# A fifth K-tile pair in seven block products in three of the four column passes of a down projection

## The chip, the cores and the metric

The kernel runs on one core of a Trainium2 chip. The metric is the time of one execution in microseconds on the device, the median of several runs. Trace times count from the start of the span of one profiled execution.

## The reference

A decoder layer on x of 256 tokens by 2048 channels in float32: a token mixer, then a channel mixer, each as x + post_norm(f(pre_norm(x))). The change lies in the channel mixer, and there in the last product:

```
h = rmsnorm(x, pre_ffn_g)
u = causal_dwconv(h @ w_up, conv_w, conv_b)          # 2048 -> 2 * 5632
gate, val = split(u, 2)
y = (gelu(gate) * val) @ w_down                      # 5632 -> 2048
x = x + rmsnorm(y, post_ffn_g)
```

## The kernel before

Every float32 operand of a matmul is split into a high part (a float32r cast, on ACT) and a low part (the rest, a subtraction on DVE), and a product is three matmuls: left high with right high, left high with right low, left low with right high. `split` (lines 311 to 313) makes the parts of the down projection's weights: the cast is L312, the subtraction L313. They go into the tiles whi and wlo, of which there are five each (`WB = 5`).

The hidden dimension of 5632 is done in two halves of 22 K-tiles of 128. A half first runs the up projection, the convolution and the gate for its 22 K-tiles, whose results stay as G (22 tiles, 256 tokens, high and low parts), and then its down projection: two column passes, n = 0 and n = 2, of 1024 output columns each. So there are four passes in all, two in each half. A pass goes through the 11 pairs of K-tiles, called pair 0 to pair 10 here. For a pair the two weight tiles ra and rb (128 rows by 1024 columns) are loaded; with two blocks of 128 tokens and two blocks of 512 columns a pair is a product of 2 x 2 by 2 x 2 blocks.

- A **plain** pair makes the eight block products as they stand: 24 matmuls with a moving operand of 512 columns, into four banks (late: p2, p3, p4, p22, one for each block of the result). It needs the parts of ra and rb: two casts and two subtractions, 1024 wide.
- A **fast** pair (those in FAST) makes seven block products, Winograd's form of Strassen's method: 21 matmuls, into the four late banks and four early ones (m1, m5, m7, m6). It needs sums of the token blocks, made once for each half by `token_sums` right after G and kept in sums, and differences of the weight blocks, made on DVE in each pass: t13 (L1007, L1008) and t24 (L1011, L1013), four operations 512 wide, in tb. It then splits b11 (half of ra, 512 wide), t13 into f13, t24 into f24 and rb into b2 (1024 wide). PE uses them in the order b11 (m1), f13 (m5, m7), f24 (m6, p4), b2 (p2, p3); in each product the high part comes first, the low part second.

The order of pairs is a table: 1, 3, 0, 5, 2, 7, 4, 8, 6, 9, 10 in a half's first pass and 0 to 10 in its second. After the last fast pair `add_early` adds the early banks to y_sb (four adds on DVE after a copy on ACT in half 0, L1116 to L1119; eight in half 1, L1123 to L1130). The last pair's products go block by block, and each block of the result is added to y_sb when it is done (L1149 in half 0; L1087 in half 1, with a square on ACT behind it). The last pass of all holds back its last three pairs (HOLD) and mixes them with the closing norm.

Weights are loaded by SP into eight places in turn: five raw tiles, two places in the tile extra, one in tb. tb shares its room with the tiles of the convolution ("room"), so it can be filled only when the half's convolution is over. Only PE's order is written out in this part of the code; the order on DVE, ACT, POOL and SP is set by a scheduler when the program is built.

Of the kernel before, what the change touches and what calls it, by code (L numbers as in the profile page):

```python
# [8 lines left out]
F32 = mybir.dt.float32  # L9
F32R = mybir.dt.float32r  # L10
BF16 = mybir.dt.bfloat16
AF = mybir.ActivationFunctionType
ALU = mybir.AluOpType
# [4 lines left out]
P = 128  # L18
S = 256
D = 2048  # L20
# [5 lines left out]
FHALF = 22  # L26
HOLD = 3
FAST = (0, 2, 4, 6)


@with_exitstack
def hybrid_layer(ctx: ExitStack, tc: tile.TileContext, x, pre_mix_g, w_in, b_forget, sinks,
# [31 lines left out]
    UNIT = 1024  # L64
# [782 lines left out]
    with tc.tile_pool(name="ffn", bufs=1) as fp:  # L847
# [105 lines left out]
        def token_sums(into, y0, y1):  # L953

            s = fp.tile([P, 4, P], F32, tag="cst", name="s")
            a11, a21 = y0[:, 0:P], y0[:, P:256]
            a12, a22 = y1[:, 0:P], y1[:, P:256]
            dve.tensor_tensor(s[:, 0, :], a21, a22, op=ALU.add)
            dve.tensor_tensor(s[:, 2, :], a11, a21, op=ALU.subtract)
            dve.tensor_tensor(s[:, 1, :], s[:, 0, :], a11, op=ALU.subtract)  # L960
            dve.tensor_tensor(s[:, 3, :], a12, s[:, 1, :], op=ALU.subtract)
            split(into[:, 0:512], into[:, 512:UNIT], s.rearrange("p k c -> p (k c)"))
# [6 lines left out]

        def fast_pass(G, sums, order, k00, c0, load, tb, early, late, add_early, hold=1,  # L970
                      keep=None):

            left, right = slice(0, 512), slice(512, UNIT)
            fast = [u for u in order if u in FAST]

# [18 lines left out]
            for u in order:  # L994
                k = 2 * u
                ra, rb = (load(w_rows(w_down, k00 + k + a, 1, c0, UNIT)) for a in range(2))
                if u in FAST:
                    i = FAST.index(u)
                    end = u == fast[-1]

                    def s_of(j):
                        return (sums[:, i, j * P:(j + 1) * P],
                                sums[:, i, 512 + j * P:512 + (j + 1) * P])

# [44 lines left out]
        for half in range(2):  # L1049
# [4 lines left out]
            for g in range(FHALF // 2):  # L1054
# [24 lines left out]
                if g in FAST:  # L1079
                    if sums is None:  # L1080
                        sums = main.tile([P, len(FAST), UNIT], F32R, tag="x", name="sums")
                    token_sums(sums[:, FAST.index(g), :], *ys)

# [5 lines left out]

            extra = fp.tile([P, 2, UNIT], F32, tag="gbc", name="extra")  # L1090
            tb = fp.tile([P, 3, UNIT], F32, tag="room", name="tb")
            spare = [extra[:, 0, :], extra[:, 1, :], tb[:, 2, :]]
            loads = [0]
# [9 lines left out]
            for n in (0, 2):  # L1103
                early, late = ([bank(tag) for _ in range(4)] for tag in ("acc", "att"))
                order = list(range(FHALF // 2))
                if n == 0:
                    order[:9] = [1, 3, 0, 5, 2, 7, 4, 8, 6]

# [25 lines left out]
                if final:  # L1134
                    rest = main.tile([P, 2, 2, UNIT], F32R, tag="hT", name="rest")
                block = fast_pass(G, sums, order, half * FHALF, n * 512, load, tb, early, late,
                                  add_early, HOLD if final else 1,
# [13 lines left out]
        def gain(t, n, h=None, into=None):  # L1151
            cs = slice(0, 512) if h is None else slice(h * 256, h * 256 + 256)
            ys = y_sb[:, t, n * 512:(n + 1) * 512][:, cs]
            pool.tensor_tensor(ys if into is None else into, ys,
                               gbf[:, n * 512:(n + 1) * 512][:, cs], op=ALU.mult)

# [24 lines left out]
        for t in range(2):  # L1181
            sp.dma_start(x_back[:, t, :], x_dram[t * P:(t + 1) * P, :])
        gbf = fp.tile([P, D], F32, tag="gbc", name="gbc_ffn")
        sp.dma_start(gbf, post_ffn_g[0].partition_broadcast(P))
        gain(0, 0)
# [61 lines left out]
```

## Time and profile before

| | us |
|---|---|
| median of three runs (1063.74 to 1064.3) | 1063.96 |
| the profiled execution | 1064.31 |
| its span | 1062.6 |
| PE busy | 1049.6 |
| DVE busy | 839.7 |
| ACT busy | 639.1 |
| down projection, half 0, first pass, from | 580.26 |
| half 1, first pass, from | 936.94 |

PE's busy time counts each matmul until it has drained, and these overlap; what one costs is the step from its start to the next one's. In a row of the order in time stand start, duration, engine, line, operation and how many were merged, and in square brackets how long the engine had been idle and what released it.

### The profile page before, as it was taken

The numbers are of one execution on the slowest core, as the hardware profiler recorded it, in microseconds if no ns is written. First come the engines' busy times: TensorE is split into PE (matmuls) and PEld (weight loads), VectorE is DVE, ScalarE is ACT, GpSimd is POOL, SyncE is SP. The second block draws the span as 40 slices with busy tenths as digits, with TensorE's granted clock in tenths as the row PEclk, the third lists the DMA queues.
The fourth block names the chain that finished last, engine by engine and source line by source line (L and its number), as shares of the span: only waits on it lengthen the run. The fifth ranks groups of instructions, "written<-read, shape, count | busy, mean of one in ns | idle before, by whom it ended". The sixth has DMA issues, their size and how long they took to land.

```text
span 1062.6 us, 16272 instructions
## 1 busy us (share of the span) xinstructions
PE 1049.6 (99%) x5890; PEld 914.6 (86%) x5890; DVE 839.7 (79%) x1369; ACT 639.1 (60%) x1096; POOL 229.3 (22%) x256
## 2 busy tenths in 40 slices
PE   9999999999999999999999999999999999999996
PEld 7889988888889888888888888888888888888885
DVE  5988887887467887787767999668778687789987
ACT  6767667776556765566655556446556565556551
POOL 4253335441022121211212000002121121200004
PEclk9999999999999999999999999999999999999998
DMA  8745566555773876656665666666566665656563
GB/s 280 217 120 168 162 209 202 165 170 162 282 236 107 280 231 187 193 180 185 211 188 188 193 204 206 213 196 190 169 209 188 197 197 180 194 179 200 194 242 121
DMA packets 154285, 207.08 MB, mean 195 GB/s; under 512 B 6845, under 2 KB 131037, under 8 KB 153181
## 3 DMA queue, kind: packets, MB, share of 16 engines
q1 hardware_dynamic: 153200, 203.37, 60.7%
q10 hardware_dynamic: 1004, 2.68, 0.6%
q8 instruction: 46, 0.75, 0.3%
q14 instruction: 35, 0.28, 0.1%
HBM read 201.68 MB, written 4.21 MB: 194 GB/s over the span
## 4 chain that ended last, share of the span: by engine, by line
PE 84%; DVE 9%; issue 2%; DMA 2%; ACT 2%; POOL 1%; DVEq 0%; SPq 0%; POOLq 0%; ACTq 0%
PE bank_acc L284 15%; PE bank_att L284 14%; PE bank_acc L309 12%; PE bank_att L967 9%; PE bank_acc L290 8%; PE bank_att L290 7%; PE bank_acc L253 7%; DVE wlo L313 4%; PE bank_acc L258 4%; PE bank_acc L967 2%; PE bank_att L475 1%; PE bank_att L510 1%; DVE wlo L115 1%; PE bank_acc L932 1%; DMA raw<-in_w_down_dram 1%
## 5 line engine op out<-in xcount | busy, mean ns | idle before, releaser
L115 DVE TENSOR_TENSOR wlo<-raw,whi 128x1024 fp32r<-128x1024 f32 (+3 forms) x271 | 328.5, 1224 | 127.0 <-ACT whi L112 118.4
L112 ACT CAST whi<-raw 128x1024 fp32r<-128x1024 f32 (+3 forms) x270 | 273.2, 1029 | 131.8 <-issue 88.8
L899 POOL TENSOR_TENSOR room<-room,rowf 128x256 f32<-128x256 f32 x88 | 100.3, 1160 | 393.9 <-DVE room L898 392.0
L284 PE MATMUL bank_acc<-hT,whi 128*128 128x512 f32 x736 | 173.3, 390 | 0.0
L284 PEld LDWEIGHTS bank_acc<-hT,whi 128*128 128x128 f32 x736 | 136.4, 188 | 27.4
L967 PE MATMUL bank_att<-whi,G 128*128 128x512 f32 x488 | 156.0, 389 | 0.0
L284 PE MATMUL bank_att<-hT,whi 128*128 128x512 f32 x640 | 150.6, 390 | 0.0
L284 PEld LDWEIGHTS bank_att<-hT,whi 128*128 128x128 f32 x640 | 118.7, 188 | 23.9
L967 PEld LDWEIGHTS bank_att<-whi,G 128*128 128x128 f32 x488 | 91.6, 188 | 18.9
L967 PE MATMUL bank_att<-wlo,G 128*128 128x512 f32 x244 | 95.0, 389 | 0.2 <-DVE wlo L313 0.2
L290 PEld LDWEIGHTS bank_acc<-hT,wlo 128*128 128x128 f32 x736 | 89.3, 188 | 2.0
L290 PE MATMUL bank_acc<-hT,wlo 128*128 128x256 f32 x736 | 89.8, 279 | 0.0
L901 ACT ACTIVATE room<-room,cw 128x256 f32<-128x256 f32 x88 | 53.0, 602 | 60.6 <-POOL room L899 60.6
L253 PE MATMUL bank_acc<-hT,whi 128*128 128x512 f32 x352 | 88.0, 395 | 0.0
L309 PE MATMUL bank_acc<-whi,oT 128*128 128x512 f32 (+1 forms) x272 | 81.7, 379 | 0.0
L290 PEld LDWEIGHTS bank_att<-hT,wlo 128*128 128x128 f32 x640 | 77.6, 188 | 1.7
L290 PE MATMUL bank_att<-hT,wlo 128*128 128x256 f32 x640 | 77.9, 279 | 0.0
L903 DVE SCALAR_TENSOR_TENSOR room<-room,cw 128x256 f32<-128x256 f32 x88 | 62.4, 709 | 17.6 <-ACT room L901 17.3
L253 PEld LDWEIGHTS bank_acc<-hT,whi 128*128 128x128 f32 x352 | 63.3, 188 | 11.5
L313 DVE TENSOR_TENSOR wlo<-raw,whi 128x1024 fp32r<-128x1024 f32 (+1 forms) x56 | 61.3, 1119 | 12.1 <-ACT whi L312 12.1
L312 ACT CAST whi<-tb 128x1024 fp32r<-128x1024 f32 x42 | 44.0, 1050 | 43.0 <-PE bank_att L967 19.6
L312 ACT CAST whi<-raw 128x1024 fp32r<-128x1024 f32 (+1 forms) x56 | 52.3, 958 | 27.1 <-PE bank_att L967 20.6
(254 smaller groups left out, 1594.0 us busy)
## 6 DMA issues: line engine op xcount, KB each, us to landing
raw<-in_w_up_dram SPq DMA_DIRECT2D x176, 512.0 KB, 4.2
raw<-in_w_down_dram SPq DMA_DIRECT2D x58, 512.0 KB, 4.7
raw<-in_w_in_dram SPq DMA_DIRECT2D x51, 512.0 KB, 4.7
raw<-in_w_out_dram SPq DMA_DIRECT2D x32, 512.0 KB, 4.6
extra<-in_w_down_dram SPq DMA_DIRECT2D x20, 512.0 KB, 4.7
raw<-in_w_in_dram SPq DMA_DIRECT2D x16, 384.0 KB, 3.6
tb<-in_w_down_dram SPq DMA_DIRECT2D x10, 512.0 KB, 3.5
cb<-c_dram SPq DMA_DIRECT2D x8, 256.0 KB, 3.8
```

The lines of the kernel that those rows point to most:

```text
L112: i1 = act.copy(hi[:, cs], raw[:, cs])
L115: i2 = dve.tensor_tensor(lo[:, cs], raw[:, cs], hi[:, cs].bitcast(F32), op=ALU.subtract)
L253: pe.matmul(b, parts[u][0][:, a, m * P:(m + 1) * P], hT[:, kt, :], start=(kt == 0), stop=(kt == KT - 1))
L284: pe.matmul(b, parts[u][0][:, a, m * P:(m + 1) * P], hT[:, kt, :], start=(kt == 0), stop=(kt == KT - 1))
L290: pe.matmul(b[:, 256:512], parts[u][1][:, a, m * P:(m + 1) * P], hT[:, kt, 0:256], start=False, stop=False)
L309: pe.matmul(b, a, r[:, cols], start=(first and i == 0), stop=(last and i == 2))
L312: act.copy(hi, src)
L313: dve.tensor_tensor(lo, src, hi.bitcast(F32), op=ALU.subtract)
L899: pool.tensor_tensor(u[:, 2:258], u[:, 2:258], rowf, op=ALU.mult)
L901: act.activation(y, u[:, 2:258], AF.Identity, bias=cw[:, 3, ch:ch + 1], scale=cw[:, 2, ch:ch + 1])
L903: dve.scalar_tensor_tensor(y, u[:, 1:257], cw[:, 1, ch:ch + 1], y, op0=ALU.mult, op1=ALU.add)
L967: pe.matmul(b[:, to] if to else b, a, r[:, cols], start=(first and i == 0), stop=(last and i == 2))
```

## The change

Pair 8 joins FAST. It is done in seven products in both passes of half 0 and in the first pass of half 1, while the last pass keeps four fast pairs. The first passes' order becomes 1, 3, 0, 5, 2, 7, 4, 9, 6, 8, 10: pairs 6 and 8 stand side by side, and add_early follows pair 8, with pair 10 alone behind it. The fifth pair's token sums get a tile of their own (sum5). Of the loads' three spare places one is in extra and two in tb now. The closing gain vector lies in two tiles and is loaded in two transfers.

```diff
--- before.py
+++ after.py
@@ -25,7 +25,7 @@
 NEG = -1e30
 FHALF = 22
 HOLD = 3
-FAST = (0, 2, 4, 6)
+FAST = (0, 2, 4, 6, 8)
 
 
 @with_exitstack
@@ -967,11 +967,11 @@
                 pe.matmul(b[:, to] if to else b, a, r[:, cols], start=(first and i == 0),
                           stop=(last and i == 2))
 
-        def fast_pass(G, sums, order, k00, c0, load, tb, early, late, add_early, hold=1,
+        def fast_pass(G, sums, some, order, k00, c0, load, tb, early, late, add_early, hold=1,
                       keep=None):
 
             left, right = slice(0, 512), slice(512, UNIT)
-            fast = [u for u in order if u in FAST]
+            fast = [u for u in order if u in some]
 
             def of(k, t):
                 return G[k][:, t * P:(t + 1) * P], G[k][:, 256 + t * P:256 + (t + 1) * P]
@@ -994,13 +994,13 @@
             for u in order:
                 k = 2 * u
                 ra, rb = (load(w_rows(w_down, k00 + k + a, 1, c0, UNIT)) for a in range(2))
-                if u in FAST:
-                    i = FAST.index(u)
+                if u in some:
+                    i = some.index(u)
                     end = u == fast[-1]
 
                     def s_of(j):
-                        return (sums[:, i, j * P:(j + 1) * P],
-                                sums[:, i, 512 + j * P:512 + (j + 1) * P])
+                        return (sums[i][:, j * P:(j + 1) * P],
+                                sums[i][:, 512 + j * P:512 + (j + 1) * P])
 
                     b11 = parts(ra[:, left], 512)
                     t13, t24 = tb[:, 0, :], tb[:, 1, :]
@@ -1077,9 +1077,13 @@
                     split(gt[:, 0:256], gt[:, 256:512], y)
                     ys.append(y)
                 if g in FAST:
-                    if sums is None:
-                        sums = main.tile([P, len(FAST), UNIT], F32R, tag="x", name="sums")
-                    token_sums(sums[:, FAST.index(g), :], *ys)
+                    i = FAST.index(g)
+                    if i == 0:
+                        first4 = main.tile([P, 4, UNIT], F32R, tag="x", name="sums")
+                        sums = [first4[:, n, :] for n in range(4)]
+                    elif i == 4:
+                        sums.append(fp.tile([P, UNIT], F32R, tag="sum5", name="sum5"))
+                    token_sums(sums[i], *ys)
 
             def down(t, n, b, h=None):
                 i, cs = (n, slice(0, 512)) if h is None else (n + h, slice(h * 256, h * 256 + 256))
@@ -1087,9 +1091,9 @@
                 dve.tensor_tensor(ys, b[:, cs], ys, op=ALU.add)
                 act.activation(junk[:, cs], ys, AF.Square, accum_out=ysq[t][:, i:i + 1])
 
-            extra = fp.tile([P, 2, UNIT], F32, tag="gbc", name="extra")
-            tb = fp.tile([P, 3, UNIT], F32, tag="room", name="tb")
-            spare = [extra[:, 0, :], extra[:, 1, :], tb[:, 2, :]]
+            extra = fp.tile([P, UNIT], F32, tag="extra", name="extra")
+            tb = fp.tile([P, 4, UNIT], F32, tag="room", name="tb")
+            spare = [extra, tb[:, 2, :], tb[:, 3, :]]
             loads = [0]
 
             def load(src):
@@ -1102,9 +1106,9 @@
 
             for n in (0, 2):
                 early, late = ([bank(tag) for _ in range(4)] for tag in ("acc", "att"))
-                order = list(range(FHALF // 2))
+                order, fast = list(range(FHALF // 2)), FAST[:4 if half and n else 5]
                 if n == 0:
-                    order[:9] = [1, 3, 0, 5, 2, 7, 4, 8, 6]
+                    order = [1, 3, 0, 5, 2, 7, 4, 9, 6, 8, 10]
 
                 def y_of(t, c):
                     return y_sb[:, t, (n + c) * 512:(n + c + 1) * 512]
@@ -1133,7 +1137,7 @@
                 rest = None
                 if final:
                     rest = main.tile([P, 2, 2, UNIT], F32R, tag="hT", name="rest")
-                block = fast_pass(G, sums, order, half * FHALF, n * 512, load, tb, early, late,
+                block = fast_pass(G, sums, fast, order, half * FHALF, n * 512, load, tb, early, late,
                                   add_early, HOLD if final else 1,
                                   rest and [[rest[:, a, i, :] for i in range(2)]
                                             for a in range(2)])
@@ -1152,7 +1156,7 @@
             cs = slice(0, 512) if h is None else slice(h * 256, h * 256 + 256)
             ys = y_sb[:, t, n * 512:(n + 1) * 512][:, cs]
             pool.tensor_tensor(ys if into is None else into, ys,
-                               gbf[:, n * 512:(n + 1) * 512][:, cs], op=ALU.mult)
+                               gbf[n // 2][:, n % 2 * 512:(n % 2 + 1) * 512][:, cs], op=ALU.mult)
 
         def before_last(t, n):
 
@@ -1180,8 +1184,9 @@
         x_back = main.tile([P, 2, D], F32, tag="x", name="x_back")
         for t in range(2):
             sp.dma_start(x_back[:, t, :], x_dram[t * P:(t + 1) * P, :])
-        gbf = fp.tile([P, D], F32, tag="gbc", name="gbc_ffn")
-        sp.dma_start(gbf, post_ffn_g[0].partition_broadcast(P))
+        gbf = [fp.tile([P, UNIT], F32, tag=tag, name="gbc_ffn") for tag in ("extra", "sum5")]
+        for i, g in enumerate(gbf):
+            sp.dma_start(g, post_ffn_g[0, i * UNIT:(i + 1) * UNIT].partition_broadcast(P))
         gain(0, 0)
         gain(0, 1)
         block(0)
```

Lines behind the diff's places move: L1087 becomes L1091, L1116 to L1119 become L1120 to L1123, L1123 to L1130 become L1127 to L1134, L1149 becomes L1153; L1007 to L1013, L312 and L313 keep their numbers.

On DVE, where half 1's first pass ends and pair 0 of the second pass is prepared, before (y_sb from s or bank_acc is add_early, y_sb from bank_att a block's add, wlo from extra b11 of pair 0, wlo from tb its f13 and then its f24, tb from raw a difference for pair 2):

```order
L1127 TENSOR_TENSOR s<-bank_acc,s 128x512
L313 TENSOR_TENSOR wlo<-extra,whi 128x512
L1128 TENSOR_TENSOR y_sb<-s,y_sb 128x512
L313 TENSOR_TENSOR wlo<-tb,whi 128x1024
L1129 TENSOR_TENSOR s<-bank_acc,s 128x512
L1087 TENSOR_TENSOR y_sb<-bank_att,y_sb 128x512
L1130 TENSOR_TENSOR y_sb<-s,y_sb 128x512
L1087 TENSOR_TENSOR y_sb<-bank_att,y_sb 128x512
L313 TENSOR_TENSOR wlo<-tb,whi 128x1024
L1087 TENSOR_TENSOR y_sb<-bank_att,y_sb 128x512
L1007 TENSOR_TENSOR tb<-raw 128x512
L1087 TENSOR_TENSOR y_sb<-bank_att,y_sb 128x512
```

There pair 0's four differences stood further up; f24 comes ahead of the last two block adds.

The same place now, from the middle of add_early on:

```order
L1131 TENSOR_TENSOR s<-bank_acc,s 128x512
L1091 TENSOR_TENSOR y_sb<-bank_att,y_sb 128x512
L1132 TENSOR_TENSOR y_sb<-s,y_sb 128x512
L1091 TENSOR_TENSOR y_sb<-bank_att,y_sb 128x512
L1133 TENSOR_TENSOR s<-bank_acc,s 128x512
L1091 TENSOR_TENSOR y_sb<-bank_att,y_sb 128x512
L1134 TENSOR_TENSOR y_sb<-s,y_sb 128x512
L313 TENSOR_TENSOR wlo<-tb,whi 128x1024
L1091 TENSOR_TENSOR y_sb<-bank_att,y_sb 128x512
L1011 TENSOR_TENSOR tb<-tb 128x512
L1008 TENSOR_TENSOR tb<-raw 128x512
L1013 TENSOR_TENSOR tb<-tb 128x512
```

b11 and one difference of pair 0 stand further up; f13 comes behind the whole of add_early and three block adds, and the other two differences of pair 0 (L1011, L1013), from which f24 is made, behind the fourth, with one of pair 2 (L1008) between them.

On DVE at the same place of half 0, before:

```order
L1118 TENSOR_TENSOR y_sb<-bank_acc,y_sb 128x512
L1119 TENSOR_TENSOR y_sb<-bank_acc,y_sb 128x512
L313 TENSOR_TENSOR wlo<-extra,whi 128x512
L313 TENSOR_TENSOR wlo<-tb,whi 128x1024
L1007 TENSOR_TENSOR tb<-raw 128x512
L1008 TENSOR_TENSOR tb<-raw 128x512
L1149 TENSOR_TENSOR y_sb<-bank_att,y_sb 128x512
L313 TENSOR_TENSOR wlo<-tb,whi 128x1024
L1149 TENSOR_TENSOR y_sb<-bank_att,y_sb 128x512
L1011 TENSOR_TENSOR tb<-raw,tb 128x512
L1149 TENSOR_TENSOR y_sb<-bank_att,y_sb 128x512
L1013 TENSOR_TENSOR tb<-raw,tb 128x512
```

f24 of pair 0 comes behind the first block add.

And now:

```order
L313 TENSOR_TENSOR wlo<-tb,whi 128x512
L1122 TENSOR_TENSOR y_sb<-bank_acc,y_sb 128x512
L1123 TENSOR_TENSOR y_sb<-bank_acc,y_sb 128x512
L1153 TENSOR_TENSOR y_sb<-bank_att,y_sb 128x512 x2
L313 TENSOR_TENSOR wlo<-tb,whi 128x1024
L1153 TENSOR_TENSOR y_sb<-bank_att,y_sb 128x512 x2
L1011 TENSOR_TENSOR tb<-tb 128x512
L1008 TENSOR_TENSOR tb<-raw 128x512
L1013 TENSOR_TENSOR tb<-tb 128x512
L1007 TENSOR_TENSOR tb<-raw 128x512
L313 TENSOR_TENSOR wlo<-tb,whi 128x1024 x2
L313 TENSOR_TENSOR wlo<-raw,whi 128x1024 x2
```

All four block adds stand ahead of pair 0's last differences and so of its f24.

On SP, at the start of half 1's down projection (the first place in extra is filled early, among the up projection's loads), before:

```order
L1100 DMA extra<-in_w_down_dram 128x1024 x2
L69 DMA raw<-in_w_up_dram 128x4x256 x87
L69 DMA raw<-in_w_down_dram 128x1024 x9
L1100 DMA tb<-in_w_down_dram 128x1024
L69 DMA raw<-in_w_down_dram 128x1024
L1100 DMA extra<-in_w_down_dram 128x1024 x2
L1100 DMA tb<-in_w_down_dram 128x1024
```

And now:

```order
L1104 DMA extra<-in_w_down_dram 128x1024
L69 DMA raw<-in_w_up_dram 128x4x256 x87
L69 DMA raw<-in_w_down_dram 128x1024 x9
L1104 DMA tb<-in_w_down_dram 128x1024 x2
L69 DMA raw<-in_w_down_dram 128x1024
L1104 DMA extra<-in_w_down_dram 128x1024
L1104 DMA tb<-in_w_down_dram 128x1024 x2
```

One of the two loads into extra has become a second one into tb, which waits for the convolution's room.

## The prediction

> **What bounds the kernel now.** I read the page first, then who waits for whom on PE, then the four column passes of the down projection as stretches, then the order in time of DVE, ACT and PE where one pass follows another.
>
> ```profile
> span 1062.6 us, 16272 instructions
> PE 1049.6 (99%) x5890; PEld 914.6 (86%) x5890; DVE 839.7 (79%) x1369; ACT 639.1 (60%) x1096; POOL 229.3 (22%) x256
> ...
> PE bank_acc L169 <- DVE junk L164: 1.3, 1, 1.3
> PE bank_att L522 <- DVE pl L313: 0.5, 1, 0.5
> ...
> PE bank_att L967 <- DVE wlo L313: 0.2, 1, 0.2
> ...
> 580.26:637.38 57.12, 57.12 (x253) 47.30 (x252) 53.98 (x70) 31.13 (x37) 1.79 (x2) 1.00 0.60 199
> 637.38:694.50 57.12, 57.12 (x253) 47.30 (x252) 44.49 (x48) 30.02 (x32) 0.20 (x4) 1.00 0.64 209
> 936.94:994.06 57.12, 57.12 (x253) 47.30 (x252) 54.23 (x70) 32.15 (x41) 1.79 (x2) 1.00 0.59 197
> 994.06:1050.70 56.64, 56.47 (x261) 46.94 (x260) 50.24 (x59) 28.27 (x36) 9.05 (x7) 1.00 0.50 181
> ```
>
> PE is busy 99% and waits 0.2 us in all for the down projection's parts, so each matmul removed is time gained and each new wait of PE is time lost. The last rows are the four passes (stretch, PE, PEld, DVE busy): in the first pass of either half DVE, which makes the low parts, is itself busy 53.98 and 54.23 of 57.12 us. It has 3.1 and 2.9 us free there.
>
> **What the change takes from PE.**
>
> ```profile
> 591.14 0.39 PE L967 MATMUL bank_acc<-whi,G 128*128 128x512 f32 x1
> ...
> 595.90 0.39 PE L967 MATMUL bank_att<-whi,G 128*128 128x512 f32 x1
> ...
> 601.34 0.39 PE L967 MATMUL bank_acc<-whi,G 128*128 128x512 f32 x1
> ```
>
> These are the first matmuls of pairs 0 (seven products), 5 (eight) and 2. Pair 0 takes 595.90 - 591.14 = 4.76 us for 21 matmuls, pair 5 takes 5.44 us for 24: 0.227 us each (the 0.39 is how long one is under way, not the step). Pair 8 loses three matmuls in three passes: 9 x 0.227 = 2.04 us, all on the path. That is the whole gain.
>
> **What it adds to DVE.**
>
> ```profile
> 972.95 1.23 DVE L313 TENSOR_TENSOR wlo<-tb,whi 128x1024 fp32r<-128x1024 f32 x1 [0.47 <-ACT whi L312]
> 975.48 0.69 DVE L1007 TENSOR_TENSOR tb<-extra 128x512 f32<-128x512 f32 x1 [1.31 <-DMA extra<-in_w_down_dram]
> ...
> 979.10 1.22 DVE L313 TENSOR_TENSOR wlo<-raw,whi 128x1024 fp32r<-128x1024 f32 x1
> 980.23 0.69 DVE L1013 TENSOR_TENSOR tb<-tb 128x512 f32<-128x512 f32 x1
> 980.83 1.22 DVE L313 TENSOR_TENSOR wlo<-raw,whi 128x1024 fp32r<-128x1024 f32 x1
> 981.97 0.69 DVE L1123 TENSOR_TENSOR y_sb<-s,y_sb 128x512 f32<-128x512 f32 x1
> ...
> 988.38 0.68 DVE L313 TENSOR_TENSOR wlo<-extra,whi 128x512 fp32r<-128x512 f32 x1
> 988.98 0.68 DVE L1128 TENSOR_TENSOR y_sb<-s,y_sb 128x512 f32<-128x512 f32 x1
> ...
> 993.11 1.22 DVE L313 TENSOR_TENSOR wlo<-tb,whi 128x1024 fp32r<-128x1024 f32 x1
> ...
> 996.05 1.21 DVE L313 TENSOR_TENSOR wlo<-tb,whi 128x1024 fp32r<-128x1024 f32 x1
> 997.18 1.22 DVE L313 TENSOR_TENSOR wlo<-raw,whi 128x1024 fp32r<-128x1024 f32 x1
> ```
>
> DVE from pair 6, the last fast pair of the first pass, to pair 0 of the second pass. Start to start, a 1024-wide operation takes 1.14 us and a 512-wide one 0.60. A plain pair costs DVE two of the first, 2.27 us; a fast one costs three, and five of the second (b11 and the four differences), 6.4 us. Pair 8 thus adds 4.1 us to DVE in each of three passes and gives it 0.68 us less time. Between the rows at 980.23 and 997.18 DVE never rests: seven wide and fifteen narrow operations, 7 x 1.135 + 15 x 0.60 = 16.95. Twelve of the narrow ones are adds of finished sums into y_sb: eight of add_early and one for each of the four blocks. How late is it there already?
>
> ```profile
> 994.06 0.39 PE L967 MATMUL bank_acc<-whi,G 128*128 128x512 f32 x1
> ...
> 996.33 0.39 PE L967 MATMUL bank_acc<-wlo,sums 128*128 128x512 f32 x1
> ...
> 997.69 0.39 PE L967 MATMUL bank_att<-wlo,G 128*128 128x512 f32 x1
> ...
> 639.00 1.22 DVE L313 TENSOR_TENSOR wlo<-tb,whi 128x1024 fp32r<-128x1024 f32 x1
> ...
> 641.01 0.39 PE L967 MATMUL bank_att<-wlo,G 128*128 128x512 f32 x1
> ```
>
> Pair 0's last low part, b2, is done at 997.18 and first used at 997.69 (half 1), done at 639.00 + 1.14 = 640.14 and used at 641.01 (half 0). The slack is 0.5 and 0.9 us. Before, pairs 9 and 10, both plain, stood between the last fast pair and this point; now only pair 10 does.
>
> **Can DVE run ahead?**
>
> ```profile
> 973.22 1.05 ACT L312 CAST whi<-tb 128x1024 fp32r<-128x1024 f32 x1 [0.31 <-PE bank_att L967]
> 975.90 1.06 ACT L312 CAST whi<-raw 128x1024 fp32r<-128x1024 f32 x1 [1.63 <-PE bank_att L967]
> ...
> 988.82 1.05 ACT L312 CAST whi<-tb 128x1024 fp32r<-128x1024 f32 x1 [1.66 <-PE bank_att L967]
> ```
>
> Each cast waits for PE to release one of the five whi buffers, so hardly. And DVE keeps its order: the cast of pair 6's f24 ended at 974.27, but its low part stood behind the difference that waited for a load until 975.48.
>
> Now the walk by the new order, with time 0 at pair 8's first matmul (983.18 in half 1's first pass: 936.94 + 41.48 for five plain and three fast pairs, + 4.76 for pair 6). From 974.09, where pair 6's f13 is done, eleven DVE operations lead to pair 8's b2: 5 x 1.135 + 6 x 0.60 = 9.3, and two waits of 0.5 for casts, because pair 9's last buffer comes free at 978.42; so b2 is done at +1.2. Loads don't stop DVE there any more: pair 8's lie in raw places filled long before. Pair 10's first part waits for its cast to 1.35. PE leaves pair 8 at 4.76, ends pair 10's blocks at 6.12, 7.48, 8.84 and 10.20, and then starts pair 0 of the second pass: m1, m5 (f13's low part due at 11.11), m7, m6 (f24's high part at 12.24, its low part at 12.47).
>
> Half 1. Ahead of f13's low part now stand pair 10's two wide operations, eleven adds, b11 and one difference: 1.35 + 2 x 1.135 + 13 x 0.60 = 11.4. It is done at 12.6, 1.5 us late. Behind it come the last block add, which has waited for block 4 of pair 10, and three differences, one of them for pair 2: 15.0. On ACT the cast of f24 stands behind four squares, the last one of that block add, done by 13.9; so it starts at 15.1 and ends at 16.15, and the low part at 17.35. PE, 1.5 us late, wants the high part at 13.75: 2.4 us of wait, and 1.0 more for the low part. Sum: 4.9 us.
>
> Half 0, where add_early has four adds on DVE. Two wide and eight narrow operations lead to f13: 1.35 + 2.27 + 4.8 = 8.5, its low part is done at 9.6, in time. Two block adds follow, the second held until block 4 ends (10.4): 11.0; three differences: 12.8; the cast of f24: 13.95; its low part: 15.15. PE waits 1.8 for the high part (due at 12.24, seen at 14.05) and 0.9 for the low one: 2.7 us.
>
> In half 0's second pass pair 8 is followed by 9 and 10, both plain, and DVE has 12.6 us free (57.12 - 44.49): nothing. **Sum: -2.0 + 4.9 + 2.7 = +5.6 us.**
>
> Bounds: if DVE could use all its idle time, half 1 lacks 4.1 + 0.6 (the moved difference) + 0.7 - 0.5 - 2.9 = 2.0 and half 0 4.1 + 0.6 + 0.7 - 0.9 - 3.1 = 1.4, so +1.4 in all; if it can use none, 4.9 and 4.5, so +7.4. I take the walk, since it keeps to the order and the buffers.
>
> **The small edits, costed at nothing.**
>
> ```profile
> 724.96 0.28 DVE L961 TENSOR_TENSOR s<-room,s 128x128 f32<-128x128 f32 x1
> ...
> 726.30 0.69 DVE L313 TENSOR_TENSOR sums<-s,sums 128x512 fp32r<-128x512 f32 x1
> ...
> 936.46 1.23 DVE L313 TENSOR_TENSOR wlo<-raw,whi 128x1024 fp32r<-128x1024 f32 x1 [2.85 <-ACT whi L312]
> ...
> 943.25 0.33 SPq L1100 DMA_DIRECT2D tb<-in_w_down_dram  x1
> ...
> DMA to landing us min/median/max: 3.5/3.5/6.0
> ...
> 1040.68 3.00 POOL L1154 TENSOR_TENSOR y_sb<-y_sb,gbc_ffn 128x512 f32<-128x512 f32 x2 [100.80 <-DMA gbc_ffn<-in_post_ffn_g_dram]
> ```
>
> The fifth token sums (four 0.2 us operations, one of 0.60 and a cast, once per half) go beside the up projection, where DVE rests up to 2.85 us a time; if that cover were gone they would cost 1.4 us a half. One more load waits for the conv room at a half's start (943.25); landing in 3.5 to 6.0 us it is there by 949.9, its cast by 951.0, and pair 5 starts on PE at 936.94 + 15.64 = 952.58: 1.6 us of cover. SP only keeps two more loads behind that release, none due sooner. In the second passes one raw place is now tb's, freed by pair 0's b2 and wanted for pair 4's difference: 0 to 0.6 us. The gain vector in two transfers lands no later than one.
>
> **Rivals.** (1) The adds give way and the gain stays: DVE's delay falls on y_sb, which nobody waits for, and f13 and f24 are in time. Then -2.0: 1061.9. It decides if f24's low part is done before 12.47 in half 1, five us earlier than walked. For it speaks PE's bare 0.2 us of waits now; against it the slack of 0.5 us and the rows in order. (2) The waits cost more, by the clock:
>
> ```profile
> 1051.19 0.88 PE L967 MATMUL bank_acc<-rest,G 128*128 128x256 f32 x6
> ...
> 1050.00:1055.00 5.00, 2.07 (x18) 1.86 (x16) 3.70 (x9) 1.74 (x6) 2.33 (x3) 1.00 0.51 195
> 1055.00:1058.00 3.00, 0.00 (x0) 0.00 (x0) 2.39 (x3) 0.00 (x0) 1.24 (x2) 0.51 0.10 41
> ```
>
> After PE's last matmul ended at 1052.07 the granted clock stayed 1.00 to 1055 and was 0.51 from there: about 3 us of rest halve it. My longest wait is 2.4 us, with three matmuls and 1.0 us of wait around it. Were it halved, the nine matmuls left of pair 0 would take 2.0 us more at each of the two places: +9.7, 1073.7. The Trainium skill ("TensorE: Matmul & The Clock Gate", Part 1) has the clock halved after an idle window of about 3.4 us that runs free of the kernel; by that rule a 2.4 us wait is safe, and 3.4 us with one matmul inside it may not be. (3) DVE runs further ahead than the ring lets it in my walk, say because casts start sooner after PE's release, and uses all its idle time: the lower bound, +1.4, 1065.4. Against it stand the 1.63 us that a cast waited for PE in the rows above.
>
> **How the numbers follow.** The profiled execution took 1064.31, 1.7 more than its span; the median of the runs is 0.35 lower, so 1063.96 + 5.6 = 1069.6. Chances: the walk 0.74, the clock 0.11, the lower bound 0.10, no waits 0.05. The range runs from the lower bound, 1063.96 + 1.4 = 1065.4, to a little beyond the upper bound, 1071.4, for one of two clock drops: 1072.6. A measurement of this kernel can tell about 0.2%, 2.1 us: slower by more 0.88 (the first two, and a third of the lower bound's), within it 0.09 (the rest of that, and half of rival 1, whose -2.0 lies at the edge), faster 0.03.
>
> **What would show it.** PE's list of waits should hold L967 waiting for DVE wlo and ACT whi of L312, about 7.6 us, near the starts of the two second passes and nowhere else; the first passes 56.4 us instead of 57.12; L967 nine matmuls fewer; DVE without a gap in those places. Wrong would be: no such waits, waits inside the first passes (pairs 6 and 8 side by side), or a granted clock under 1.00 there.

## The result, and the profile after

| | before | after |
|---|---|---|
| median, us | 1063.85 (6 runs, 1063.37 to 1064.30) | 1072.26 (6 runs, 1069.84 to 1074.45) |
| ratio of the times | | 1.0078, interval 1.0062 to 1.0094 |
| profiled execution, us | 1064.31 | 1073.85 |
| its span, us | 1062.6 | 1072.1 |

The change made the kernel 8.4 us slower, where 5.6 was forecast. The runs of after lie in three groups, each with its mean granted clock: 1069.84 and 1070.10 (0.996), 1072.18 and 1072.33 (0.994), 1073.85 and 1074.45 (0.991). The profiled execution is one of the last group.

The head of the page, and then who PE waits for (total, times, longest, in us):

```profile
span 1072.1 us, 16302 instructions
PE 1053.4 (98%) x5881; PEld 916.4 (85%) x5881; DVE 854.8 (80%) x1397; ACT 645.2 (60%) x1104; POOL 228.8 (21%) x256
```

```profile
PE bank_acc L967 <- ACT whi L312: 3.8, 2, 2.1
PE bank_acc L967 <- DVE wlo L313: 2.7, 3, 1.5
```

Nine matmuls fewer, 5881 for 5890, and 6.5 us of waits for the down projection's parts where there were 0.2. Where they are, in PE's order in time; first the start of half 0's second pass, then that of half 1's:

```profile
638.19 0.39 PE L967 MATMUL bank_acc<-whi,sums 128*128 128x512 f32 x1
640.28 0.50 PE L967 MATMUL bank_acc<-whi,sums 128*128 128x512 f32 x1 [1.70 <-ACT whi L312]
641.54 0.79 PE L967 MATMUL bank_acc<-wlo,sums 128*128 128x512 f32 x1 [0.76 <-DVE wlo L313]
642.13 0.63 PE L967 MATMUL bank_acc<-whi,sums 128*128 128x512 f32 x1
642.56 0.63 PE L967 MATMUL bank_att<-whi,G 128*128 128x512 f32 x1
...
1000.15 0.50 PE L967 MATMUL bank_acc<-wlo,sums 128*128 128x512 f32 x1 [1.46 <-DVE wlo L313]
1003.69 0.80 PE L967 MATMUL bank_acc<-whi,sums 128*128 128x512 f32 x1 [2.10 <-ACT whi L312]
1004.95 0.80 PE L967 MATMUL bank_acc<-wlo,sums 128*128 128x512 f32 x1 [0.46 <-DVE wlo L313]
```

These are the places of the forecast, f24's high and low part in half 0, f13's low part and both of f24's in half 1, and there are no others: no row of L967 inside a first pass has a wait. The reader should also see the steps behind the waits: from 642.13 to 642.56 a matmul takes 0.43 us, where it took 0.227 before.

DVE in half 1, from f13's low part (998.87) to f24's (1003.67):

```profile
998.87 1.23 DVE L313 TENSOR_TENSOR wlo<-tb,whi 128x1024 fp32r<-128x1024 f32 x1
1000.00 0.69 DVE L1091 TENSOR_TENSOR y_sb<-bank_att,y_sb 128x512 f32<-128x512 f32 x1
1000.60 0.69 DVE L1011 TENSOR_TENSOR tb<-tb 128x512 f32<-128x512 f32 x1
1001.20 0.70 DVE L1008 TENSOR_TENSOR tb<-raw 128x512 f32<-128x512 f32 x1
1001.80 0.70 DVE L1013 TENSOR_TENSOR tb<-tb 128x512 f32<-128x512 f32 x1
1002.40 0.70 DVE L1007 TENSOR_TENSOR tb<-raw 128x512 f32<-128x512 f32 x1
1003.67 2.36 DVE L313 TENSOR_TENSOR wlo<-tb,whi 128x1024 fp32r<-128x1024 f32 x2 [0.56 <-ACT whi L312]
```

It is the row of work that the walk counted: the last block add (L1091), three differences, of which one (L1008) is for the next fast pair, and then the wait for the cast. The fourth difference (L1007), which the walk did not have, falls into the time of that cast and so costs nothing; 0.56 us of the cast are left behind it.

The granted clock stands in the column ahead of the last two (stretch, its length, busy time of PE, PEld, DVE, ACT and POOL, PEclk, DMA share, GB/s). First after, half 0; then a kernel with the same two waits there (e2, below), in an execution in which the clock held:

```profile
642.00:648.00 6.00, 6.00 (x16) 4.61 (x16) 6.00 (x8) 2.63 (x4) 0.00 (x0) 0.53 0.57 175
```

```profile
642.00:648.00 6.00, 6.00 (x28) 4.97 (x27) 6.00 (x9) 2.17 (x3) 0.00 (x0) 1.00 0.63 195
```

From 640.87, inside the second wait, the clock of after was half for 6.8 us; in the stretch shown 16 matmul records stand where e2 has 28. In half 1 it was half from 1002.68 on, again for 6.8 us.

To tell the parts apart in each run, three lengths were read off each trace: the start of half 0's first pass; from there to half 1's first pass (before 936.94 - 580.26 = 356.68 us); and from there to DVE's last row (before 121.52). For half 1 these are the rows, of before and then of after, with the first of the closing 256-column matmuls:

```profile
1047.59 0.28 PE L967 MATMUL bank_acc<-whi,G 128*128 128x256 f32 x1
1058.46 0.47 DVE L1173 SCALAR_TENSOR_TENSOR y_sb<-last,ry,x_back 128x256 f32<-128x256 f32 x1
```

```profile
1057.99 0.28 PE L967 MATMUL bank_acc<-whi,G 128*128 128x256 f32 x1
1068.11 0.47 DVE L1177 SCALAR_TENSOR_TENSOR y_sb<-last,ry,x_back 128x256 f32<-128x256 f32 x1
```

Differences to before, in us:

| profiled execution | start | half 0 | half 1 | both halves |
|---|---|---|---|---|
| after | -0.32 | +4.56 | +5.41 | +9.97 |
| e12, after again | -1.22 | +3.15 | +4.84 | +7.99 |
| e1, fifth pair in half 0's second pass | -0.77 | -0.68 | +0.63 | -0.05 |
| e2, in half 0's first pass | -0.70 | +2.36 | +0.66 | +3.02 |
| e3, in half 1's first pass | -0.77 | +0.05 | +5.75 | +5.80 |
| e4, waits filled | -1.02 | +1.70 | +3.27 | +4.97 |
| e5, small edits alone | -0.66 | 0.00 | +0.55 | +0.55 |
| e6, seven adds left out | -0.81 | +1.67 | -2.09 | -0.42 |
| e7, differences on POOL | -0.40 | +0.87 | +3.38 | +4.25 |
| e8, and adds on POOL | +0.05 | +0.87 | +2.41 | +3.28 |
| e9, DVE's order | -0.73 | -0.91 | +4.87 | +3.96 |
| e10, order and sums | -0.96 | -0.95 | -0.49 | -1.44 |
| e11, two plain pairs behind | -0.04 | -0.49 | +1.88 | +1.39 |

The start differs from one execution to the next by up to 1.3 us, ahead of all the code that was touched.

### The profile page after: what moved, and what is told of

It is laid out like the page before. It is cut to its first block, busy times and chain, and to the rows that moved or that the text cites. A ratio compares the mean times of both kernels' runs of the same rounds, so it can differ in the third digit from the quotient of the medians.

```text
span 1072.1 us, 16302 instructions
## 1 busy us (share of the span) xinstructions
PE 1053.4 (98%) x5881; PEld 916.4 (85%) x5881; DVE 854.8 (80%) x1397; ACT 645.2 (60%) x1104; POOL 228.8 (21%) x256
## 4 chain that ended last, share of the span: by engine, by line
PE 92%; DVE 4%; ACT 1%; issue 1%; DMA 1%; POOL 1%; DVEq 0%; SPq 0%; POOLq 0%; ACTq 0%
PE bank_acc L284 16%; PE bank_att L967 15%; PE bank_att L284 14%; PE bank_acc L309 12%; PE bank_acc L290 8%; PE bank_att L290 7%; PE bank_acc L253 7%; PE bank_acc L967 4%; PE bank_acc L258 4%; PE bank_att L475 1%; PE bank_att L510 1%; DVE wlo L115 1%; PE bank_acc L932 1%; DVE wlo L313 1%; PE bank_att L534 1%
## 5 line engine op out<-in xcount | busy, mean ns | idle before, releaser
L967 PE MATMUL bank_att<-whi,G 128*128 128x512 f32 x452 | 148.1, 395 | 0.0
L967 PEld LDWEIGHTS bank_att<-whi,G 128*128 128x128 f32 x452 | 86.5, 191 | 18.3
L312 ACT CAST whi<-tb 128x1024 fp32r<-128x1024 f32 (+1 forms) x58 | 58.0, 1012 | 59.1 <-DVE tb L1013 34.7
L967 PE MATMUL bank_att<-wlo,G 128*128 128x512 f32 x226 | 89.2, 395 | 0.0
L313 DVE TENSOR_TENSOR wlo<-tb,whi 128x1024 fp32r<-128x1024 f32 (+1 forms) x58 | 67.4, 1176 | 9.6 <-ACT whi L312 9.5
L313 DVE TENSOR_TENSOR wlo<-raw,whi 128x1024 fp32r<-128x1024 f32 (+1 forms) x56 | 60.3, 1101 | 11.8 <-ACT whi L312 11.8
```

The lines of the kernel that those rows point to most:

```text
L312: act.copy(hi, src)
L313: dve.tensor_tensor(lo, src, hi.bitcast(F32), op=ALU.subtract)
L967: pe.matmul(b[:, to] if to else b, a, r[:, cols], start=(first and i == 0), stop=(last and i == 2))
```

## The experiments

The theory: DVE comes late to the second passes, because pair 8's work now lies so near them. The rivals: the loads and rooms; pairs 6 and 8 side by side; and the clock, as a cost on top. Each ratio below is to before, on the same chip; there were four chips (e1 to e4; e5 to e8; e9 to e11; e12), and before's median on them was 1063.9 to 1064.5.

**One pass at a time.** e1 to e3 give FAST's fifth pair to one pass each. From after:

```diff
-order, fast = list(range(FHALF // 2)), FAST[:4 if half and n else 5]
+order, fast = list(range(FHALF // 2)), FAST[:5 if half == 0 and n else 4]          # e1
+order, fast = list(range(FHALF // 2)), FAST[:5 if half == 0 and n == 0 else 4]     # e2
+order, fast = list(range(FHALF // 2)), FAST[:5 if half and n == 0 else 4]          # e3
```

with the first pass's order of before wherever pair 8 is plain.

> The change with the fifth pair only in half 0's second pass; the first passes have four fast pairs in the order of before, and rooms, raw places and the fifth token sums are as after. Late DVE: DVE has 12.6 us free in that pass and two plain pairs follow pair 8, so there is no wait: three matmuls fewer, -0.7 us, and a granted clock of 1.00 throughout. If the rooms or raw places cause the waits: the 2.5 and 4.0 us of PE waits stay, +5 us or more.

Measured: 1063.10, ratio 0.9990 (0.9982 to 0.9999). Half 0 is 0.68 us shorter in the trace, three matmuls to the digit, and L967 waits for nothing.

> The fifth pair only in half 0's first pass, with the new order there; the rest as in before. Late DVE: -0.7 for three matmuls, +2.5 for the two waits at the start of half 0's second pass, none in half 1: +1.8 with a full clock, and about +4.0 in executions in which the clock drops there (2.2 a drop), so runs in two groups, not three. If the waits of the two halves were one cause (a shared one, say the loads): waits in both halves or in neither.

Measured: 1067.81, ratio 1.0034 (1.0021 to 1.0048). The profiled execution kept its clock (the row of e2 above): half 0 took +2.36, and half 1 had no new wait. The waits were 1.70 and 0.76, as in after. The runs' mean clocks were 0.994 to 0.996, so some of five had a drop; the two groups that were expected don't show in the times (1066.5 to 1068.8), and the median is 3.5 us over before's.

> The fifth pair only in half 1's first pass, with the new order there; the rest as in before. Late DVE: -0.7 for three matmuls, +4.0 for the three waits at the start of half 1's second pass: +3.3 with a full clock, about +5.5 where the clock drops; two groups, not three. If the waits of the two halves were one cause: waits in both halves or in neither.

Measured: 1069.08, ratio 1.0045 (1.0032 to 1.0058), mean clock 0.993 to 0.995 in all five. Its waits:

```profile
PE bank_acc L967 <- ACT whi L312: 2.1, 1, 2.1
PE bank_acc L967 <- DVE wlo L313: 1.9, 2, 1.5
```

4.0 us, half 1's share of after's 6.5, and none in half 0. So the waits belong to the first pass that carries pair 8, each on its own, and the loads that both kernels share don't make them. The time came out 0.7 us under the one forecast for a run with a drop, and no run kept its clock.

**The small edits alone.** Four fast pairs everywhere (`FAST[:4]`), the orders of before, the rest of the change kept.

> Everything of the change except the fifth pair in products: four fast pairs and the order of before in all passes, but the rooms, raw places, the fifth token sums (made and not used) and the gain vector in two transfers as after. Late DVE: no waits of L967 and the time of before, within 0.5 us. If the loads into tb's places or the rooms cause the waits at the starts of the second passes: 6.5 us of waits as in after.

Measured: 1064.27, ratio 1.0006 (0.9997 to 1.0015): not told from nothing. The trace has 0.55 us more in half 1, and no wait of L967 at the starts of the second passes. The rooms and raw places don't cause the waits.

**The waits filled with matmuls.** In pair 0 of the second passes:

```diff
+                    if fill and u == 0:
+                        for _ in range(10):
+                            pe.matmul(m6, s_of(0)[0], f13[0][:, left], start=True, stop=True)
                     product(m6, *s_of(1), f24, left, first(m6), end)
```

> After, with ten more matmuls in pair 0 of each second pass, ahead of f24's first product: they write into m6's bank, which that product then starts anew, so nothing of the result changes, and they need only parts that are there already. The waits for f24 (1.7 and 0.8 us in half 0, 2.1 and 0.5 in half 1) are filled by 2.3 us of matmuls each. If the rest of PE makes the clock drop: no drop or at least fewer (half 1 keeps the wait of 1.5 us for f13), all runs near after's fastest, 1069.9 to 1070.5. If the drop has nothing to do with PE's rest: runs up to 1074.5 as with after. If the waits are not DVE's lateness but PE's own: ten matmuls twice add 4.5 us, 1074.5 without a drop.

Measured: 1068.60, ratio 1.0039 (1.0026 to 1.0051), all five runs at a mean clock of 0.997. PE in half 0:

```profile
637.72 2.43 PE L1022 MATMUL bank_acc<-whi,sums 128*128 128x512 f32 x10
639.99 0.39 PE L967 MATMUL bank_acc<-whi,sums 128*128 128x512 f32 x1
640.85 0.50 PE L967 MATMUL bank_acc<-wlo,sums 128*128 128x512 f32 x1 [0.48 <-DVE wlo L313]
```

Ten matmuls more (L1022), and half 0 is as long as in e6 below, which has the same waits unfilled and a full clock: +1.70 beside +1.67. So PE had that time to spare, and the end is set by DVE.

**After once more**, on another chip:

> The changed kernel once more, for the clock. If waits alone made its time: every run at before + 5 to 6 us, since the waits are the same in each. If a drop of the clock comes on top in some executions: runs spread over before + 5 (mean granted clock 0.996 to 0.997) to before + 9.5 (0.991 to 0.992), the mean clock falling by about 0.001 for each us, and the median 2 to 4 us above that of e4, which has the same waits filled with matmuls.

Measured: 1070.98 (1069.35 to 1072.25), ratio 1.0064 (1.0051 to 1.0078). Four of five runs have a mean clock of 0.993 or 0.994 and take 1070.4 to 1072.3; the fifth, at 0.996, takes 1069.35. The median lies 6.75 us over its before, e4's 4.28 over its own: 2.5 us apart. The waits are those of after (its longest 2.11), but the drop in half 0 was shorter:

```profile
642.00:648.00 6.00, 6.00 (x24) 4.80 (x23) 6.00 (x8) 2.10 (x4) 0.00 (x0) 0.85 0.70 223
```

0.85 of full speed in this stretch where the first profile had 0.53. With e4 this is shown: PE's rest brings the clock down, in most executions though not in all, and for a time that varies. What decides it stands in the last section.

**Less work for DVE.** In half 1's first pass add_early returns after its first add.

> After, without seven of the eight adds that add_early gives DVE in half 1's first pass (the output lacks those sums). Late DVE: 7 x 0.60 = 4.2 us less ahead of f13 there, so the 1.5 us wait for f13 goes; the last block add, which waits for block 4, and the differences behind it stay ahead of f24, so half 1's waits come to half 0's 2.5 us: 1.5 us less than after, with drops of the clock as in after. If the load on DVE doesn't matter (a late load, or pairs 6 and 8 side by side): 4.0 us of waits in half 1 as in after.

Measured: 1064.37, ratio 1.0003 (0.9993 to 1.0012). Two of the twelve runs have a mean clock of 0.993 or 0.994, the others 0.996 to 0.998. All of half 1's waits were gone, not 1.5 us of them. DVE's order shows why:

```profile
988.30 0.68 DVE L313 TENSOR_TENSOR wlo<-tb,whi 128x512 fp32r<-128x512 f32 x1
988.90 0.68 DVE L1008 TENSOR_TENSOR tb<-tb 128x512 f32<-128x512 f32 x1
989.50 0.68 DVE L1011 TENSOR_TENSOR tb<-tb 128x512 f32<-128x512 f32 x1
990.22 0.69 DVE L1013 TENSOR_TENSOR tb<-tb 128x512 f32<-128x512 f32 x1
990.83 0.68 DVE L1091 TENSOR_TENSOR y_sb<-bank_att,y_sb 128x512 f32<-128x512 f32 x1
991.43 1.22 DVE L313 TENSOR_TENSOR wlo<-tb,whi 128x1024 fp32r<-128x1024 f32 x1
```

With fewer adds the scheduler put the differences (L1008, L1011, L1013) ahead of the block adds (L1091). The expectation had kept the old order. So the load on DVE matters, but this run can't say how much of it was load and how much order; e9 asks that.

**Order alone.** The same work; the block adds get a lower priority in the scheduler:

```diff
                 for i in range(4):
                     block(i)
+                for i in range(4):
                     t, c = divmod(i, 2)
+                    late_add = tc.high_priority(offset=-60)
+                    late_add.__enter__()
                     ...
+                    late_add.__exit__(None, None, None)
```

> After with the same work, and only DVE's order changed at the starts of the second passes: the block adds have a lower priority, so pair 0's differences and f24's low part come ahead of the block adds that wait for PE. Late DVE, by the walk in the new order: half 0's f24 low part is done at 12.4 for 12.47, no wait; half 1's f13 in time, f24's low part at 13.65 for 12.47, 1.2 us of wait, no drop of the clock: before - 2.0 + 1.2 = -0.8 us. If it is the amount of DVE's work and not its order: 6.5 us of waits as after. If the banks of the late adds hold PE instead: new waits for DVE y_sb of up to 2 us.

Measured: 1068.77, ratio 1.0036 (1.0023 to 1.0050). In half 0 the waits went: half 0 took 0.91 us less than before, so there the order was all of it. In half 1 the wait for f13 went, that for f24's high part shrank from 2.10 to 0.38, and its low part was waited for 0.76 us. A new wait came, the rival that was put at "up to 2 us", and it was longer than that:

```profile
999.68 0.77 PE L967 MATMUL bank_att<-whi,G 128*128 128x512 f32 x1 [2.69 <-DVE y_sb L1091]
```

```profile
1000.00:1005.00 5.00, 5.00 (x13) 3.85 (x13) 4.96 (x8) 4.56 (x10) 0.00 (x0) 0.50 0.72 246
```

PE stood for the bank that p2 takes, whose add (L1091) had been put behind f24, b2 and pair 1's parts. The clock was 0.50 for the next 5 us, and the mean clock 0.994 or 0.995 in all five runs. In half 1 the order only chooses which part comes late; DVE has too much to do there.

**Work moved to POOL.** `de` is POOL for pair 0 of the second passes, DVE otherwise, and makes the four differences:

```diff
+                    de = pool if u == 0 and c0 else dve
-                    dve.tensor_tensor(t13[:, left], ra[:, right], ra[:, left], op=ALU.subtract)
+                    de.tensor_tensor(t13[:, left], ra[:, right], ra[:, left], op=ALU.subtract)
                     ...
```

> After, with the four differences of pair 0 in both second passes made on POOL, which has nothing else to do there (4 x 1.5 us by its row, ready some 4 us before f13 is due). Late DVE: 4 x 0.60 = 2.4 us less on DVE at each place, so half 0's waits go; in half 1 f24's low part comes after eleven adds, some 0.6 us late, and b2 some 0.4 late: 0.6 to 1.0 us of waits in all, no drop of the clock, before - 2.0 + 0.8 = -1.2 us. If POOL slows DVE by what they share: less than that, up to half of after's waits left. If it is not DVE: no change against after.

Measured: 1068.11, ratio 1.0036 (1.0024 to 1.0048). PE waited 0.77 and 0.46 us in half 0, 2.45 and 1.76 in half 1, 5.4 of after's 6.5: POOL slows DVE, by more than expected. The clock held, 0.996 to 0.997 in all runs, and so the time lies under after's. Half 1:

```profile
982.26 2.38 POOL L1008 TENSOR_TENSOR tb<-tb 128x512 f32<-128x512 f32 x1 [41.90 <-DVE wlo L313]
983.62 4.35 DVE L313 TENSOR_TENSOR wlo<-raw,whi 128x1024 fp32r<-128x1024 f32 x2
...
989.60 2.28 DVE L313 TENSOR_TENSOR wlo<-extra,whi 128x1024 fp32r<-128x1024 f32 x1
```

POOL takes about 2.3 us for one of these, where the estimate had 1.5, and beside it a 1024-wide low part takes DVE 2.2 us and more (4.35 for two, 2.28 for one) for 1.14 to 1.2.

e8 adds private sums in half 1's first pass (z, shown under e10), with POOL adding them to y_sb.

> e7 and, in half 1's first pass, the early and late banks summed in four tiles of their own (four adds by add_early and four block adds on DVE instead of twelve), with POOL adding those to y_sb later. Late DVE: 2.4 us less again, no waits of L967, no drop of the clock, the nine matmuls' gain in full: before - 2.0 us, faster than both kernels. If POOL's work beside DVE slows it: waits of 1 to 2 us left in half 1.

Measured: 1067.88, ratio 1.0036 (1.0024 to 1.0048). Half 1 still has five waits, 2.7 us in all, above the 1 to 2 expected. One pair of rows shows which work of DVE suffers:

```profile
989.65 2.15 POOL L1014 TENSOR_TENSOR tb<-tb 128x512 f32<-128x512 f32 x1
990.58 0.68 DVE L1131 TENSOR_TENSOR z<-bank_acc,z 128x512 f32<-128x512 f32 x1
```

An add that reads a bank and one tile takes its usual 0.68 us in the middle of POOL's 2.15.

**Where pair 8 stands.** `order = [1, 3, 0, 5, 2, 7, 4, 6, 8, 9, 10]` in the first passes.

> After with pair 9 behind pair 8 in the first passes (4, 6, 8, 9, 10 in place of 4, 9, 6, 8, 10): the same work, three fast pairs side by side and two plain ones behind them. If the waits come from pair 10 alone standing behind pair 8: the slack at the second pass is that of before plus a little, so the waits there go, and DVE's lateness shows inside the first pass instead, ahead of pair 8 (b11 or f13 some 2 us late in either half, since three fast pairs side by side cost DVE 19.2 us in 14.3 of PE's): 3 to 4 us of waits in all, before + 1.5, no or few drops of the clock. If the sum of DVE's work in the pass alone decides: waits as large as after's, 6.5 us.

Measured: 1065.43, ratio 1.0007 (0.9998 to 1.0017). Three fast pairs side by side made no wait inside the first passes. At the second passes 0.18 us is left in half 0 and 2.34 in half 1. DVE in half 1's first pass, of e11 and then of after (PE, PEld, DVE busy):

```profile
936.41:992.85 56.44, 56.44 (x250) 46.73 (x249) 55.66 (x73) 31.77 (x41) 1.79 (x2) 1.00 0.61 201
```

```profile
941.18:997.62 56.44, 56.44 (x250) 46.77 (x249) 54.59 (x71) 32.36 (x40) 1.79 (x2) 1.00 0.63 208
```

With the fast pairs earlier DVE fits 55.66 us of work into the pass for 54.59, and takes that much less over the edge. Both parts of the expectation missed the waits: the lateness did not move into the pass, and it did not stay as large. The time, 0.9 us over before for 1.5, came near all the same.

**Order and sums: a version that beats both.** e9's priorities, and in half 1's first pass:

```diff
+z = main.tile([P, 4, 512], F32, tag="hT", name="z")
+zs.extend(z[:, i, :] for i in range(4))
+act.copy(zs[0], m1)
+dve.tensor_tensor(zs[3], m6, zs[0], op=ALU.add)
+dve.tensor_tensor(zs[1], m5, zs[3], op=ALU.add)
+dve.tensor_tensor(zs[2], m7, zs[3], op=ALU.add)
+dve.tensor_tensor(zs[3], m5, zs[2], op=ALU.add)
+return
 ...
-                        down(t, n + c, late[i])
+                        dve.tensor_tensor(zs[i], late[i], zs[i], op=ALU.add)
+                        put.append((t, c, zs[i]))
```

and `down(t, c, z)` for each of `put`, behind pair 2 of the last pass. The tile rest is made only when pair 10 needs it.

> e9 and, in half 1's first pass, the early and late banks summed in four tiles of their own, eight adds on DVE, with the four adds to y_sb put behind pair 2 of the next pass (DVE does the same number of adds, four of them later; POOL does none). Late DVE: f13 at 8.3 for 11.1, f24's low part at 12.4 for 12.47: no waits of L967, no drop of the clock, before - 2.0 us, 1062 beside 1064, the fastest. If banks or casts hold PE: 1 us of waits left, before - 1.0.

Measured: 1062.38 (11 runs, 1061.62 to 1063.44) beside 1064.50, ratio 0.9981 (0.9972 to 0.9990), clock 0.996 to 0.998. What is left of waits, and the start of half 1's second pass:

```profile
PE bank_acc L967 <- DVE wlo L313: 0.7, 1, 0.7
```

```profile
991.47:1008.00 16.53, 15.67 (x68) 12.23 (x66) 16.53 (x21) 11.29 (x17) 0.00 (x0) 1.00 0.43 145
```

One wait of 0.7 us, a full clock, and the gain of the nine matmuls. It is the fifth pair as meant: by medians 2.1 us under before on its chip, where after in e12 is 6.75 over before on its own.

## Why the prediction was right, and where it was off

- **The gain.** 2.04 us for nine matmuls, three a pass. e1 has 0.68 for one pass.
- **Half 0's waits.** Forecast 1.8 and 0.9, seen 1.70 and 0.76. But a wait costs PE more than its idle time, as e2's rows show at a full clock:

```profile
637.82 0.39 PE L967 MATMUL bank_acc<-whi,sums 128*128 128x512 f32 x1
639.90 0.50 PE L967 MATMUL bank_acc<-whi,sums 128*128 128x512 f32 x1 [1.70 <-ACT whi L312]
641.16 0.50 PE L967 MATMUL bank_acc<-wlo,sums 128*128 128x512 f32 x1 [0.76 <-DVE wlo L313]
641.50 0.39 PE L967 MATMUL bank_acc<-whi,sums 128*128 128x512 f32 x1
```

From 637.82 to 639.90 are 2.08 us, the step of 0.227 and 1.85, not 1.70: the matmul ahead drains first. From 641.16 to 641.50 are 0.34, 0.11 over a step. That makes 0.27 a wait. So 2.46 + 0.54 = 3.0 for 2.7, and -1.36 + 3.0 = +1.64 is half 0 at a full clock; e6 has +1.67.
- **Half 1's waits.** Forecast 1.5, 2.4 and 1.0, seen 1.46, 2.10 and 0.46. The last is short because the matmul ahead of it ran at half the clock (0.80 us for 0.50); e4 and e12, in which that matmul ran at the full clock, have 0.76 there. So at a full clock it is 4.32 + 3 x 0.27 = 5.1 for 4.9. Order alone did not help here: e9 has 3.8 us of waits in this place.
- **What the walk left out.** In half 1 the closing got shorter: from the first 256-column matmul to DVE's last row 10.87 us before (1047.59 to 1058.46), 10.12 after. Every kernel with pair 8 fast in half 1 has 9.8 to 10.6 there, every other one 10.9 to 11.6. Why wasn't looked into. And before's wait of 0.17 us in the last pass (0.44 with its steps) was gone. So half 1 at a full clock is -0.68 + 5.1 - 0.75 - 0.44 = +3.2, where e4 has +3.27, and both halves are +4.9, not +5.6; e4 has +4.97. That the walk came so near is in part luck: the steps beside the waits (1.35 us in all) and the shorter closing, which it left out, nearly cancel.
- **The small edits**, costed at nothing: nothing that the times can tell (e5). The traces of e1, e2 and e5, whose half 1 has four fast pairs in the order of before, are 0.55 to 0.66 us longer there, mostly in the closing; the interval of e5 neither shows nor excludes that much.
- **The clock, the term that was mis-sized.** Rival 2 had the right mechanism, 0.11 of chance, and 2.0 us a place. It came in at least eight of eleven runs of after. The profiled execution is 9.97 - 4.9 = 5.1 us over the walk with these terms, 2.9 of it in half 0 (4.56 - 1.67) and 2.1 in half 1 (5.41 - 3.27). In the run in the middle it cost some 2.5 us, by e12 and e4. The step that failed is the bound taken from the end of before's trace, "about 3 us of rest halve it", read as a limit on one rest. Here no rest was longer than 2.1 us, and 1.8 us of rest within 3.4 us, in two pieces, were enough (last section). Three runs of after, at a mean clock of 0.996, may be free of it: 1069.35 to 1070.10, 5.1 to 6.3 over before's medians; no profile shows one of them. The median of 1072.26 lies inside the range only because its upper end had been raised from 1071.4 to 1072.6 for one drop. With a chance of 0.11 for the clock, that is luck.
- **The other rivals.** The adds didn't give way by themselves (rival 1), but e10, which makes them, comes to its -2.0. The lower bound, DVE using its idle time (rival 3), is near what e11's order brings: +1.4 in the trace, though no run shows that it is for this reason.
- **"Wrong would be"**: a clock under 1.00 at those places was named as a sign of it, and it is there; waits inside the first passes were named too, and there are none. The waits that were to be seen, about 7.6 us, add to 6.5.

## What to carry to other kernels

Before giving an engine more work in one stage, count its work up to the next point at which the bottleneck waits for it, in the order in which it does it; a few free microseconds over the whole stage say little. Where a late engine's row holds operations that themselves wait for the bottleneck, move those behind what the bottleneck waits for, and take away the cause of the hurry: private sums, added later, turned 8 us lost into 2 us gained. And price a wait of TensorE above its idle time: the drain, and, where rests lie close together, a chance of 3.4 or 6.8 us at half the clock.

## What was not expected of the hardware

- **Short rests can halve the granted clock, and not every time.** Rests of 1.70 and 0.76 us with a matmul between them halved it in the profiles of after and e12 and left it at 1.00 in those of e2 and e6. In e3 (1.46, 2.1, 0.5) and e9 (0.38, 0.76, 2.69) all runs have a lower mean clock. One rest of 2.45 us between busy stretches, in e7, left it at 1.00. The traces show what decides. In each of the fourteen, all changes of the granted clock lie whole numbers of 3.41 us apart: after's two drops, for one, lie 361.8 us apart, 106 times that, and each lasts 6.83 us, e12's last 3.41. Cut at these points, half 0's start in after, then in e6, and then the rest of 2.45 us in e7:

```profile
637.45:640.87 3.42, 1.63 (x6) 0.77 (x5) 2.83 (x5) 1.69 (x2) 0.00 (x0) 1.00 0.00 0
640.87:647.69 6.82, 6.15 (x15) 4.80 (x16) 6.82 (x8) 3.76 (x5) 0.00 (x0) 0.50 0.46 140
```

```profile
636.83:640.24 3.41, 1.71 (x7) 0.91 (x5) 2.82 (x5) 1.54 (x2) 0.00 (x0) 1.00 0.00 0
640.24:643.65 3.41, 2.65 (x12) 2.18 (x12) 3.41 (x4) 3.41 (x5) 0.00 (x0) 1.00 0.11 24
```

```profile
987.05:990.47 3.42, 2.43 (x11) 1.69 (x9) 3.42 (x3) 1.05 (x1) 3.34 (x2) 1.00 0.67 232
990.47:993.88 3.41, 1.95 (x9) 1.61 (x9) 3.41 (x5) 1.04 (x1) 0.32 (x1) 1.00 0.37 129
```

In after PE rests 1.79 us within one window (3.42 less 1.63), and half the clock follows. In e6 a boundary parts the same two rests into 1.70 and 0.76, in e7 it cuts the one rest into 0.99 and 1.46, and the clock stays. So it is in all fourteen traces: each of the 20 windows at a full clock in which PE rested 1.79 us or more was followed by half the clock, and none in which it rested 1.72 or less. So rests close together add up within a window, and chance lies in where the window starts; the runs without a trace have only their mean clock. The Trainium skill ("TensorE: Matmul & The Clock Gate", Part 1) says that a free-running window of about 3.4 us is watched, and the traces agree. Its advice to keep idle gaps under about 3 us ("Why this matters for your kernels") was not enough: PE's rests at these places in after were all under 2.2 us.

- **POOL beside DVE.** DVE's operations with two operands in SBUF took about 2.2 us beside POOL for 1.14; those that read a bank weren't slowed (0.68). The Trainium skill ("SBUF — State Buffer", "Who interferes with whom") has a DVE instruction with two SBUF inputs contend with a GpSimd one that reads SBUF, and one with at most one SBUF input not. The traces agree on both. By it the gain that e7 expected was out of reach from the start, since the low parts and the differences all have two operands in SBUF.
